# One transpose fewer a head, and the sums and states of the last hand-over taken up earlier, in the mLSTM layer of a two-layer decoder step

## The chip, the core and the metric

The kernel runs on one core of one Trainium2 chip. Its time is the device time in microseconds (us) of one execution. The time before is the median of 3 runs.

## The reference

One inference step of a two-layer decoder trunk, in float32, for a prompt of 256 tokens and 8 samples of 8 new tokens each (320 tokens in all, model width 1024). Layer 0 mixes tokens with a gated MLP in chunks of 128, layer 1 with an mLSTM matrix memory of 8 heads (key width 128, value width 256); each is followed by a gated MLP with a causal convolution. Only the mLSTM layer is touched. Per head `h` it computes, cut to what matters here:

```python
sc  = einsum('bhtd,bhsd->bhts', q, k) * w_intra
num = w_inter * einsum('bhtd,bhde->bhte', q, C) + einsum('bhts,bhse->bhte', sc, v)
den = w_inter * einsum('bhtd,bhd->bht', q, n) + sum(sc, axis=-1)
h   = num / maximum(abs(den), exp(-m_t))
C_new = decay * C + einsum('bhsd,bhse->bhde', k * g, v)
...
hn = (h - mean(h)) * rsqrt(var(h) + EPS) * gn_g
o  = sigmoid(o_pre)
y  = (o * hn) @ w_out
```

The prompt starts from an empty state, each sample from its own `C`, `n` and `m`; the new states are outputs as well.

## The kernel before

All activations lie transposed in SBUF: 128 partitions hold one block of 128 features, and the 320 tokens run along the free dimension (256 of the prompt, then 64 of the samples). A projection of one 128-wide block is 24 matmuls of 128x320: each weight block is split into a high and a low part (`wh` by ScalarE at L154, `wl` by VectorE at L155), and for each of 8 input blocks there are two products with `wh` and one with `wl`. In layer 1 the products with `wl` follow those with `wh` (`low_last`).

Layer 1 (`layer_b`) goes head by head, and the work of head `h-1` is laid between the projections of head `h`. An iteration of the loop holds in this order: the q block and its epilogue (`qk_epi`), the k block, the products of the samples' queries with their states (`inter`), the numerators of head `h-1` (`numer`), the first v block, the statistics of the numerators (`stats`, which end in `sl`, one over the standard deviation, made on GpSimd), the prompt's new state (`state_prompt`), two samples' new states (`state_sample(h-1, 0)`), the second v block, `state_sample(h-1, 1)`, `normed` (the normalised sums `hn`: (num - mean) * sl), `scores`, the two o blocks with `o_epi` (tanh of the output gate), `finish(h-1)` (transposes `hn`, makes `y_b` = (tanh + 1) * hn transposed, and splits it into `yhb` and `ylb`), the loads of the next states (`state_in`), their splits into `Ch` and `Cl` (`state_split`), and the transposes of k and v (`k_nat`, `v_nat`).

In `normed` and `finish`, `hn` is a tile of three groups of 128 token rows: two of the prompt and one whose lower 64 rows hold the samples and whose upper 64 rows are zeros. `finish` makes six transposes of 128x128, three for each half `e` of the head's 256 values, into two PSUM tiles named `phn`, and one `y_b` of 128x320 for each half.

The last iteration (`h = 7`, here "the last hand-over") has no o blocks in the loop: right behind `scores(7)` comes `finish(6)`, then products of the output projection (`begin(0)`, `begin(1)`), which use the finished heads, and `state_sample(6, 2)` and `(6, 3)`. Head 7's own o blocks, `stats`, `normed` and `finish(7)` stand behind the loop.

The order on TensorE is the order of the program: every matmul and transpose is pinned. The order on the other engines is laid out when the program is built, by a planner that knows the program order, the data and an estimate of each instruction's time. `tc.issue_after(ins)` makes every instruction traced in its block that runs on the engine of `ins` stand behind `ins` on that engine; it orders nothing else. Tiles come from pools with a fixed number of buffers; in PSUM `psm` has 3 (projections) and `psa` has 5 (`phn`, `num`, `pcs`, `psc`, `pCp`, `pv` and others), and a tile waits for a buffer until the last reader of the tile that held it is done.

Of the kernel before, what the change touches and what calls it, by code (L numbers as in the profile page):

```python
# [10 lines left out]
F32 = mybir.dt.float32  # L11
F32R = mybir.dt.float32r
AF = mybir.ActivationFunctionType
# [3 lines left out]
P = 128  # L17
EPS = 1e-6
TP = 256
# [6 lines left out]
NH = 8  # L26
# [11 lines left out]
class Net:  # L38
# [597 lines left out]
    def layer_b(self):  # L636
# [5 lines left out]
        with ExitStack() as ctx:  # L642
# [220 lines left out]
            def k_nat(h):  # L863
                s = S[h]
                ks = s["k"][0]
                pool, tag = (self.psm, "pm") if h < NH - 1 else (self.psa, "pa")
                pk = pool.tile([P, 512], F32, tag=tag, name="pk")
                for t in range(3):
                    self.tr(pk[:, t * P:(t + 1) * P], ks[:, t * P:(t + 1) * P], self.ident)
                kgh = hp.tile([P, 2, P], F32R, tag="kgh", name="kgh", bufs=1)  # L870
                kgl = hp.tile([P, 2, P], F32R, tag="kgl", name="kgl", bufs=1)
                kgs = hp.tile([P, 2, P], F32R, tag="kgs", name="kgs", bufs=1)
                kgz = hp.tile([P, NB, P], F32R, tag="kgz", name="kgz", bufs=1)
                g = colsT[:, 2, 32 + h:33 + h]
                src = pk[:, 2 * P:3 * P]

                for i, (r, o) in enumerate(((slice(0, 32), slice(32, 64)), (slice(32, 64), slice(0, 32)))):
                    nc.scalar.activation(kgs[:, i, :], src, AF.Copy, scale=g)
                    nc.vector.scalar_tensor_tensor(kgs[o, i, :], src[r], g[r], kgs[r, i, :].bitcast(F32), op0=MULT, op1=SUB)
                s["kg"] = (kgh, kgl, kgs, kgz)  # L880
                if h < NH - 1:
                    k_mask(h)
                for t in range(2):
                    g = colsT[:, t, 32 + h:33 + h]
                    src = pk[:, t * P:(t + 1) * P]
                    nc.scalar.activation(kgh[:, t, :], src, AF.Copy, scale=g)
                    nc.vector.scalar_tensor_tensor(kgl[:, t, :], src, g, kgh[:, t, :].bitcast(F32), op0=MULT, op1=SUB)
# [82 lines left out]
            def normed(h):  # L970
                src, mv, sl = S[h].pop("norm")
                nb = hp.tile([P, 3], F32, tag="nb", name="nb", bufs=1)
                made = nc.vector.scalar_tensor_tensor(nb, mv[:, :, 0], -1.0, sl, op0=MULT, op1=MULT)
                if h == NH - 1:
                    self.pin(made)
                for t in range(3):
                    n = P if t < 2 else 64
                    if h == NH - 1 and t:
                        nc.vector.tensor_scalar(hn[:n, t, :], src[t][:n, :DV], mv[:n, t, 0:1], sl[:n, t:t + 1], op0=SUB, op1=MULT)
                    else:  # L980
                        nc.scalar.activation(hn[:n, t, :], src[t][:n, :DV], AF.Identity, scale=sl[:n, t:t + 1], bias=nb[:n, t:t + 1])

            def state_prompt(h):
                s = S[h]
# [9 lines left out]
            def state_sample(h, i):  # L994
                s = S[h]
                kgz, dec, C0 = s["kg"][3], s["P"][2], s["C"][i]

                wide = h < NH - 2
                pcs = [pool.tile([P, 512], F32, tag=tag, name="pcs") for pool, tag in
                       ((self.psa, "pa"), (self.psm, "pm") if wide else (self.psa, "pa"))]  # L1000
                for u in range(2):
                    b = 2 * i + u
                    mm(pcs[u][:, :CW], kgz[:, b, :], vh[:, 2, :] if b < 4 else vb, True, True)
                for u in range(2):
                    b = 2 * i + u
                    made = nc.vector.scalar_tensor_tensor(C0[:, u, :], C0[:, u, :], dec[:, b:b + 1], pcs[u][:, :CW], op0=MULT, op1=ADD)  # L1006
                nc.sync.dma_start(O["Cs"][h, :, 2 * i:2 * i + 2, :], C0)
                return made

            def o_epi(h, j, ps):  # L1010
                o = lp.tile([P, T], F32, tag="ob", name="o_b", bufs=1)
                nc.vector.tensor_tensor(o, ps[:, :T], self.rb, op=MULT)  # L1012
                th = lp.tile([P, T], F32, tag="tho", name="th_o", bufs=4)
                nc.scalar.activation(th, o, AF.Tanh, scale=0.5)
                S[h].setdefault("o", []).append(th)

            def finish(h):
                s = S[h]
                yh = hp.tile([P, 2, T], F32R, tag="yhb", name="yhb", bufs=6)
                yl = hp.tile([P, 2, T], F32R, tag="ylb", name="ylb", bufs=6)  # L1020
                for e in range(2):
                    pt = self.psa.tile([P, 512], F32, tag="pa", name="phn")
                    for t in range(3):
                        self.tr(pt[:, t * P:(t + 1) * P], hn[:, t, e * P:(e + 1) * P], self.ident)
                    y = self.tp.tile([P, T], F32, tag="yf", name="y_b", bufs=2)
                    nc.vector.scalar_tensor_tensor(y, s["o"][e], 1.0, pt[:, :T], op0=ADD, op1=MULT)
                    g = gnh[:, 2 * h + e:2 * h + e + 1]
                    nc.scalar.activation(yh[:, e, :], y, AF.Copy, scale=g)
                    nc.vector.scalar_tensor_tensor(yl[:, e, :], y, g, yh[:, e, :].bitcast(F32), op0=MULT, op1=SUB)
                    Y[2 * h + e] = (yh[:, e, :], yl[:, e, :])  # L1030
# [11 lines left out]
            vb = hp.tile([P, CW], F32R, name="vb")  # L1042
            Qz = hp.tile([P, 8 * 136], F32R, name="Qz")
            Ps = hp.tile([P, P], F32R, name="Ps")
            hn = hp.tile([P, 3, DV], F32, name="hn")
            nc.gpsimd.memset(hn[64:, 2, :], 0.0)
            nc.gpsimd.memset(vh[:, :, DV:DV + 1].bitcast(F32), 1.0)
            nc.gpsimd.memset(vh[:, :, DV + 1:].bitcast(F32), 0.0)
            nc.gpsimd.memset(vl[:, :, DV:].bitcast(F32), 0.0)
# [10 lines left out]
            def blk():  # L1060
                return self.block(KD, self.x_rhs)

            part, done = {}, {}

            def begin(m):

# [7 lines left out]
            for h in range(NH):  # L1074
                if h:
                    rows_in(h)
                    qk_epi(h, 0, blk())
                    early(h, 0)
                    if h == 1:
                        inter(0, 0)  # L1080
                        state_split(0, 3)
                    inter(h - 1, 1)
                    qk_epi(h, 1, blk())
                    for i in (2, 3):
                        inter(h - 1, i)
                    numer(h - 1)
                    early(h, 1)
                    ps = blk()
                    with self.behind_split():
                        stats(h - 1)  # L1090
                    v_epi(h, 0, ps)
                    state_prompt(h - 1)
                    state_sample(h - 1, 0)
                    early(h, 2)
                    v_epi(h, 1, blk())
                if h:
                    made = state_sample(h - 1, 1)
                    with tc.issue_after(made.ins):
                        normed(h - 1)
                scores(h)  # L1100
                early(h, 3)
                last = h == NH - 1
                if h and not last:
                    o_epi(h, 0, blk())
                if last:
                    finish(h - 1)
                    begin(0)
                if h:
                    for i in (2, 3) if last else (2,):
                        state_sample(h - 1, i)  # L1110
                if last:
                    begin(1)

                    self.prefetch(0, self.used + 2)
                early(h, 4)
                if h:
                    state_in(h)
                    with tc.issue_after(made.ins):
                        for i in (0, 1):
                            state_split(h, i)  # L1120
                if h and not last:
                    o_epi(h, 1, blk())
                if h and not last:
                    finish(h - 1)
                    state_sample(h - 1, 3)
                k_nat(h)
                v_nat(h)
                if h:
                    inter(h, 0)
                    for i in (2, 3):  # L1130
                        low = state_split(h, i)
                else:
                    with tc.issue_after(self.parts[0].ins), tc.issue_after(self.parts[1].ins):
                        state_split(0, 2)
                early(h, 5)
# [184 lines left out]
```

## Time and profile before

| | |
|---|---|
| median of 3 runs | 955.47 us (955.44 to 955.82) |
| the profiled execution | 956.29 us, of which its span is 954.3 us |
| mean granted TensorE clock | 0.999 |
| TensorE busy | 946.0 us, 99% of the span |
| VectorE, ScalarE, GpSimd busy | 697.1, 531.0, 118.6 us |
| HBM traffic over the span | 162 GB/s |

The span runs from the first instruction to the last. A row of a timeline gives start, duration, engine, line, operation, destination and sources, how many like it are merged (xN), and in brackets how long the engine sat idle just before and what ended that. PE is TensorE's matmul, PEld its weight load, DVE VectorE, ACT ScalarE, POOL GpSimd, SPq the queue that issues DMAs.

### The profile page before, as it was taken

The page shows a single profiled execution, that of the slowest core. Times are in us where ns is not written, and L with a number is a line of the kernel's source. Part 1 is how long each engine was busy: PE and PEld are TensorE (multiplying, and loading weights), DVE is VectorE, ACT ScalarE, POOL GpSimd, SP SyncE. Part 2 cuts the span into 40 slices and gives each one's busy share as a digit, 9 for nine tenths or more (in the row PEclk, how much of TensorE's full clock was granted, in tenths as well). Part 3 has the DMA queues.
Part 4 walks back from the last instruction along what each step waited for, and adds up shares of the span by engine and source line. Part 5 has one row for each costly group of instructions (what it writes and reads, how often), then busy time and mean ns, then how long its engine had stood idle before and what let it go on. Part 6 is the DMA issues. An engine that isn't in the chain of part 4 may idle for free.

```text
span 954.3 us, 17083 instructions
## 1 busy us (share of the span) xinstructions
PE 946.0 (99%) x6420; PEld 932.1 (98%) x6420; DVE 697.1 (73%) x1324; ACT 531.0 (56%) x978; POOL 118.6 (12%) x291
## 2 busy tenths in 40 slices
PE   9999999999999999999999999999999999999997
PEld 8889999999999999999999999999999999999997
DVE  5866976577777764559999998887897777775443
ACT  6657443454554443348877767666766445544342
POOL 3200000010000000014432312202001000000000
PEclk9999999999999999999999999999999999999999
DMA  8643346444444454465465756654474444445441
GB/s 262 208 162 134 129 135 202 162 141 149 153 156 151 138 160 155 146 216 175 155 198 191 222 167 205 198 188 129 123 241 155 150 145 152 155 146 154 143 141 55
DMA packets 55237, 156.13 MB, mean 164 GB/s; under 512 B 7492, under 2 KB 13132, under 8 KB 55156
## 3 DMA queue, kind: packets, MB, share of 16 engines
q1 hardware_dynamic: 55156, 155.06, 50.2%
q8 instruction: 50, 0.82, 0.3%
q14 instruction: 31, 0.25, 0.1%
HBM read 143.05 MB, written 11.99 MB: 162 GB/s over the span
## 4 chain that ended last, share of the span: by engine, by line
PE 92%; DVE 4%; ACT 2%; issue 1%; DMA 1%; SPq 0%; POOL 0%; ACTq 0%
PE pm L54 80%; PE pv_a L54 5%; PE num L54 2%; PE pmix L54 1%; DVE wl L155 1%; PE pcs L54 1%; DMA raw<-in_a_wv 1%; PE pCp L54 1%; PE phn L57 0%; ACT wh L154 0%; PE pv L57 0%; PE psc L54 0%; PE pc L54 0%; DVE C L1006 0%; DVE dg L291 0%
## 5 line engine op out<-in xcount | busy, mean ns | idle before, releaser
L154 ACT CAST wh<-raw 128x1024 fp32r<-128x1024 f32 (+3 forms) x256 | 256.7, 1004 | 276.6 <-PE pm L54 147.8
L155 DVE TENSOR_TENSOR wl<-raw,wh 128x1024 fp32r<-128x1024 f32 (+3 forms) x256 | 299.0, 1169 | 125.7 <-ACT wh L154 121.5
L54 PE MATMUL pm<-xh,wh 128*128 128x320 f32 x1216 | 372.2, 311 | 0.2 <-DVE o_b L1012 0.2
L54 PE MATMUL pm<-xl,wh 128*128 128x320 f32 x1216 | 370.2, 309 | 0.0
L54 PE MATMUL pm<-xh,wl 128*128 128x320 f32 x1216 | 321.2, 309 | 0.0
L54 PEld LDWEIGHTS pm<-xh,wh 128*128 128x128 f32 x1216 | 228.4, 188 | 0.6 <-DVE o_b L1012 0.4
L54 PEld LDWEIGHTS pm<-xl,wh 128*128 128x128 f32 x1216 | 228.4, 188 | 0.2
L54 PEld LDWEIGHTS pm<-xh,wl 128*128 128x128 f32 x1216 | 214.5, 188 | 0.0
L54 PE MATMUL pm<-yh_f,wh 128*128 128x320 f32 x352 | 108.8, 309 | 0.0
L54 PE MATMUL pm<-yl_f,wh 128*128 128x320 f32 x352 | 108.8, 309 | 0.0
L54 PE MATMUL pm<-yh_f,wl 128*128 128x320 f32 x352 | 108.8, 309 | 0.0
L54 PEld LDWEIGHTS pm<-yh_f,wh 128*128 128x128 f32 x352 | 66.1, 188 | 0.0
L54 PEld LDWEIGHTS pm<-yl_f,wh 128*128 128x128 f32 x352 | 66.1, 188 | 0.0
L54 PEld LDWEIGHTS pm<-yh_f,wl 128*128 128x128 f32 x352 | 66.1, 188 | 0.0
L532 DVE SCALAR_TENSOR_TENSOR fcv<-fpad,vecs,fcv 128x336 f32<-128x336 f32 x88 | 49.6, 566 | 2.1 <-ACT fcv L530 0.7
L54 PE MATMUL pm<-yh_a,wh 128*128 128x320 f32 x128 | 39.6, 310 | 0.0
L54 PE MATMUL pm<-yh_a,wl 128*128 128x320 f32 x128 | 39.5, 309 | 0.0
L54 PE MATMUL pm<-yl_a,wh 128*128 128x320 f32 x128 | 39.5, 309 | 0.0
L534 ACT ACTIVATE fgl<-fcv 128x256 f32<-128x256 f32 x44 | 18.3, 415 | 37.8 <-DVE fcv L532 37.8
L54 PE MATMUL pm<-yhb,wh 128*128 128x320 f32 x128 | 38.1, 311 | 0.0
L54 PE MATMUL pm<-ylb,wh 128*128 128x320 f32 x128 | 37.9, 309 | 0.0
L304 DVE TENSOR_TENSOR xT<-pm,xT 128x320 f32<-128x320 f32 x39 | 19.0, 488 | 25.0 <-PE pm L54 24.9
(289 smaller groups left out, 1368.3 us busy)
## 6 DMA issues: line engine op xcount, KB each, us to landing
raw<-in_f_up SPq DMA_DIRECT2D x88, 512.0 KB, 3.2
raw<-in_b_win SPq DMA_DIRECT2D x48, 512.0 KB, 3.9
raw<-in_f_dn SPq DMA_DIRECT2D x32, 448.0 KB, 3.3
C<-in_C SPq DMA_DIRECT2D x32, 258.0 KB, 3.8
out_Cs<-C SPq DMA_DIRECT2D x32, 258.0 KB, 3.8
raw<-in_a_win SPq DMA_DIRECT2D x16, 512.0 KB, 3.2
raw<-in_a_wo SPq DMA_DIRECT2D x16, 512.0 KB, 4.0
raw<-in_f_dn SPq DMA_DIRECT2D x16, 512.0 KB, 3.5
```

The costliest lines, as they stand in the source:

```text
L54: self.pin(self.nc.tensor.matmul(out, lhsT, rhs, start=start, stop=stop, skip_group_check=skip))
L154: self.last_split = self.hold(nc.scalar.copy(wh[:, :kn, :], raw[:, :kn, :]))
L155: self.last_low = nc.vector.tensor_tensor(wl[:, :kn, :], raw[:, :kn, :], wh[:, :kn, :].bitcast(F32), op=SUB)
L304: self.nc.vector.tensor_tensor(x, ps[:, :T], x, op=ADD)
L532: nc.vector.scalar_tensor_tensor(cv, pd[:, i:i + NC], self.vec(w + i * KF), cv, op0=MULT, op1=ADD)
L534: nc.scalar.activation(gl[:, :TP], cv[:, :TP], AF.Gelu_apprx_tanh)
```

## The change

- The samples' normalised sums go to a tile of their own, `hs`, in which the two halves `e` lie one under the other (64 rows each), so that one transpose turns both; `hn` keeps the two prompt groups. The write of the samples' sums becomes two instructions of 64x128 instead of one of 64x256. `finish` makes four transposes into one PSUM tile and one into another. The zeroing of `hn`'s upper rows goes.
- `y_b` becomes one tile for both halves, made by one instruction over 128x(2x256) for the prompt and one over 128x(2x64) for the samples. The two tanh tiles of a head become one.
- In the last iteration `normed(6)` moves up behind `state_sample(6, 0)`, ordered behind its last VectorE instruction; `state_in(7)` and the first two `state_split(7, ...)` follow there, the latter's VectorE part behind `nb` (L973). Both stand ahead of `state_sample(6, 1)` and `scores(7)`.
- In iterations from the third on, the VectorE instructions traced in the k block (the low part `wl` of a later weight block) stand behind the last `y_b`.
- Head 0's transposed k goes to a `psa` tile instead of a `psm` tile.

```diff
-                pool, tag = (self.psm, "pm") if h < NH - 1 else (self.psa, "pa")
+                pool, tag = (self.psm, "pm") if 0 < h < NH - 1 else (self.psa, "pa")
...
-                for t in range(3):
-                    n = P if t < 2 else 64
-                    if h == NH - 1 and t:
-                        nc.vector.tensor_scalar(hn[:n, t, :], src[t][:n, :DV], mv[:n, t, 0:1], sl[:n, t:t + 1], op0=SUB, op1=MULT)
+                last = h == NH - 1
+                for t in range(2):
+                    if last and t:
+                        nc.vector.tensor_scalar(hn[:, t, :], src[t][:, :DV], mv[:, t, 0:1], sl[:, t:t + 1], op0=SUB, op1=MULT)
                     else:
-                        nc.scalar.activation(hn[:n, t, :], src[t][:n, :DV], AF.Identity, scale=sl[:n, t:t + 1], bias=nb[:n, t:t + 1])
+                        nc.scalar.activation(hn[:, t, :], src[t][:, :DV], AF.Identity, scale=sl[:, t:t + 1], bias=nb[:, t:t + 1])
+
+                for e in range(2):
+                    a, z = hs[64 * e:64 * e + 64, :], src[2][:, e * P:(e + 1) * P]
+                    if last:
+                        nc.vector.tensor_scalar(a, z, mv[:64, 2, 0:1], sl[:64, 2:3], op0=SUB, op1=MULT)
+                    else:
+                        nc.scalar.activation(a, z, AF.Identity, scale=sl[:64, 2:3], bias=nb[:64, 2:3])
+                return made
...
             def finish(h):
...
+                pt, ps = [self.psa.tile([P, 512], F32, tag="pa", name="phn") for _ in range(2)]
                 for e in range(2):
-                    pt = self.psa.tile([P, 512], F32, tag="pa", name="phn")
-                    for t in range(3):
-                        self.tr(pt[:, t * P:(t + 1) * P], hn[:, t, e * P:(e + 1) * P], self.ident)
-                    y = self.tp.tile([P, T], F32, tag="yf", name="y_b", bufs=2)
-                    nc.vector.scalar_tensor_tensor(y, s["o"][e], 1.0, pt[:, :T], op0=ADD, op1=MULT)
+                    for t in range(2):
+                        self.tr(pt[:, (2 * e + t) * P:(2 * e + t + 1) * P], hn[:, t, e * P:(e + 1) * P], self.ident)
+                self.tr(ps[:, :P], hs, self.ident)
+                yb = lp.tile([P, 2, T], F32, name="y_b", bufs=1)
+                o = s["o"]
+                for c, n, x in ((slice(0, TP), TP, pt), (slice(TP, T), 64, ps)):
+                    self.y_made = nc.vector.scalar_tensor_tensor(yb[:, :, c], o[:, :, c], 1.0, x[:, :2 * n].rearrange("p (e t) -> p e t", e=2), op0=ADD, op1=MULT)
+                for e in range(2):
+                    y = yb[:, e, :]
...
-            nc.gpsimd.memset(hn[64:, 2, :], 0.0)
...
+            def states(h, made):
+
+                state_in(h)
+                with tc.issue_after(made.ins):
+                    for i in (0, 1):
+                        state_split(h, i)
...
                     inter(h - 1, 1)
-                    qk_epi(h, 1, blk())
+                    if h > 1:
+                        with tc.issue_after(self.y_made.ins):
+                            ps = blk()
+                    else:
+                        ps = blk()
+                    qk_epi(h, 1, ps)
...
-                    state_sample(h - 1, 0)
+                    made = state_sample(h - 1, 0)
                     early(h, 2)
                     v_epi(h, 1, blk())
+                last = h == NH - 1
+                if last:
+                    with tc.issue_after(made.ins):
+                        made = normed(h - 1)
+                    states(h, made)
                 if h:
                     made = state_sample(h - 1, 1)
-                    with tc.issue_after(made.ins):
-                        normed(h - 1)
+                    if not last:
+                        with tc.issue_after(made.ins):
+                            normed(h - 1)
                 scores(h)
...
-                if h:
-                    state_in(h)
-                    with tc.issue_after(made.ins):
-                        for i in (0, 1):
-                            state_split(h, i)
+                if h and not last:
+                    states(h, made)
```

More of the change, by code (lines that the diff above doesn't have):

```diff
@@ L1012, in o_epi @@
                 nc.vector.tensor_tensor(o, ps[:, :T], self.rb, op=MULT)
-                th = lp.tile([P, T], F32, tag="tho", name="th_o", bufs=4)
-                nc.scalar.activation(th, o, AF.Tanh, scale=0.5)
-                S[h].setdefault("o", []).append(th)
+                if not j:
+                    S[h]["o"] = lp.tile([P, 2, T], F32, tag="tho", name="th_o", bufs=2)
+                nc.scalar.activation(S[h]["o"][:, j, :], o, AF.Tanh, scale=0.5)
             def finish(h):
@@ L1044, in layer_b @@
             Ps = hp.tile([P, P], F32R, name="Ps")
-            hn = hp.tile([P, 3, DV], F32, name="hn")
-            nc.gpsimd.memset(hn[64:, 2, :], 0.0)
+            hn = hp.tile([P, 2, DV], F32, name="hn")
+            hs = hp.tile([P, P], F32, name="hs")
             nc.gpsimd.memset(vh[:, :, DV:DV + 1].bitcast(F32), 1.0)
@@ L1092, in layer_b @@
                     state_prompt(h - 1)
-                    state_sample(h - 1, 0)
+                    made = state_sample(h - 1, 0)
                     early(h, 2)
                     v_epi(h, 1, blk())
+                last = h == NH - 1
[3 more added lines that the diff above has]
+                    states(h, made)
                 if h:
                     made = state_sample(h - 1, 1)
-                    with tc.issue_after(made.ins):
-                        normed(h - 1)
+                    if not last:
+                        with tc.issue_after(made.ins):
+                            normed(h - 1)
                 scores(h)
                 early(h, 3)
-                last = h == NH - 1
                 if h and not last:
```

## The prediction, made before the change was run

> **What bounds the kernel now.** I read the page first, then the waits of TensorE's weight loads, the chain that ended last, and the timeline around each wait that the change can touch.
>
> ```profile
> PE 946.0 (99%) x6420; PEld 932.1 (98%) x6420; DVE 697.1 (73%) x1324; ACT 531.0 (56%) x978; POOL 118.6 (12%) x291
> PE 92%; DVE 4%; ACT 2%; issue 1%; DMA 1%; SPq 0%; POOL 0%; ACTq 0%
> PEld phn L57 <- ACT hn L981: 1.8, 3, 1.2
> PEld num L54 <- DVE y_b L1026: 0.5, 1, 0.5
> PEld pm L54 <- DVE o_b L1012: 0.4, 1, 0.4
> ```
>
> TensorE is the bound over nearly the whole span, and its order is fixed. So an edit pays only where it takes work off TensorE or one of these three waits (total us, times, longest). The first is the last hand-over; here is its timeline:
>
> ```profile
> 663.16 0.88 DVE L1006 SCALAR_TENSOR_TENSOR C<-C,Mb,pcs 128x258 f32<-128x258 f32 x2
> 663.32 0.85 POOL L964 TENSOR_TENSOR sl<-t,mhalf 128x3 f32<-128x3 f32 x1 [4.70 <-DVE t L962]
> 665.96 0.41 ACT L154 CAST wh<-raw 128x256 fp32r<-128x256 f32 x1 [2.54 <-PE pm L54]
> 666.85 0.42 DVE L155 TENSOR_TENSOR wl<-raw,wh 128x256 fp32r<-128x256 f32 x1 [2.67 <-ACT wh L154]
> 667.09 0.53 PEld L54 LDWEIGHTS psc<-qs 128*128 128x128 f32 x4
> 667.20 0.87 DVE L1006 SCALAR_TENSOR_TENSOR C<-C,Mb,pcs 128x258 f32<-128x258 f32 x2
> 668.17 1.02 ACT L981 ACTIVATE hn<-num,nb,sl 128x256 f32<-128x256 f32 x2 [0.84 <-DVE nb L973]
> 668.65 1.28 DVE L911 TENSOR_TENSOR Cl<-C,Ch 128x516 fp32r<-128x516 f32 x2
> 668.79 0.14 PEld L57 LDWEIGHTS phn<-ident,hn 128*128 128x128 f32 x1 [1.17 <-ACT hn L981]
> 669.24 0.14 PEld L57 LDWEIGHTS phn<-ident,hn 128*128 128x128 f32 x1 [0.32 <-ACT hn L981]
> 669.73 0.42 PEld L57 LDWEIGHTS phn<-ident,hn 128*128 128x128 f32 x4 [0.35 <-ACT hn L981]
> ```
>
> TensorE has loaded its last scores weight at 667.62 and stands for 1.17 + 0.32 + 0.35 = 1.84 us until `hn` arrives piece by piece. `hn` needs `sl`, there at 664.17, and `nb`, which is queued behind the second pair of C; yet VectorE had sat idle for 2.67 us and ScalarE for 2.54 us before that.
>
> **Part by part.** *Last hand-over.* Behind the first C pair (done 664.04), `nb` can run at 664.2 and ScalarE can make `hn` and `hs` from 664.4. Two operations of 0.5 us (1.02 for the pair above) and two of about 0.36 (the 128x128 row below) end near 666.1. That lies in ScalarE's idle time but for 0.15 us, by which the `wh` at 665.96 may slip. The transposes can then start at 667.62 without a wait: **-1.84 us**. Of the states that move, the loads are long issued, the `Ch` casts are ordered behind nothing new, and the two `Cl` (1.28 us of VectorE) fall into its 2.67 us of idle time; if they didn't, they would stand where they stand now. The output DMA that is passed stays behind its own C.
>
> ```profile
> 645.19 0.33 SPq L903 DMA_DIRECT2D C<-in_C  x1
> L878 ACT ACTIVATE kgs<-pk,cols 128x128 fp32r<-128x128 f32 x12 | 4.3, 360 | 0.7 <-DVE kgs L879 0.2
> L981 ACT ACTIVATE hn<-ns,nb,sl 64x256 f32<-64x256 f32 x6 | 3.6, 595 | 0.0
> 473.23 0.59 ACT L981 ACTIVATE hn<-ns,nb,sl 64x256 f32<-64x256 f32 x1
> 505.18 0.66 PE phn L57 x6
> L57 PE MATMUL phn<-ident,hn x48: 271/272/328, 476.2 to 688.4; 128*128 128x128 f32 x48
> ```
>
> *Transposes.* In the chain, six take 0.66 us of TensorE's time: 0.11 each. Eight go, one a head; head 0's stands ahead of the wait at 478.46 (below) and vanishes in it, so 7 x 0.11 = **-0.77 us**. The duration of one is 272 ns because they overlap, and is not its price. The Trainium skill (TensorE: Matmul & The Clock Gate, Part 4: PE-mode transpose) gives about 275 ns for a transpose in a kernel's context; the duration here agrees, but charged for each it would make this term 1.93 us and the sum -3.5 us. The chain's spacing decides for 0.11.
>
> *`hs` in two pieces.* 2 x 0.36 in place of 0.595 is 0.13 us more ScalarE a head, hidden because `hn` is ready ahead of its transposes: in iteration 1 at 473.82, when the first of them runs at 476.2. Uncovered it would cost just that. In `finish(7)` the two pieces run on VectorE ahead of the `hn` of ScalarE, and no wait of `phn` but that of the hand-over is in the list above.
>
> *`y_b` by parts.* The first instruction now spans 512 elements:
>
> ```profile
> L1026 DVE SCALAR_TENSOR_TENSOR y_b<-th_o,phn 128x320 f32<-128x320 f32 x14 | 6.3, 479 | 0.2 <-PE phn L57 0.2
> L832 DVE SCALAR_TENSOR_TENSOR Pf<-psc,w 128x384 f32<-128x384 f32 x5 | 2.8, 551 | 0.0
> L911 DVE TENSOR_TENSOR Cl<-C,Ch 128x516 fp32r<-128x516 f32 x24 | 15.5, 682 | 0.0
> 477.94 0.87 DVE L1026 SCALAR_TENSOR_TENSOR y_b<-th_o,phn 128x320 f32<-128x320 f32 x2
> 478.46 0.19 PEld L54 LDWEIGHTS num<-Ch,Qz 128*128 128x128 f32 x1 [0.50 <-DVE y_b L1026]
> 505.70 0.88 DVE L1026 SCALAR_TENSOR_TENSOR y_b<-th_o,phn 128x320 f32<-128x320 f32 x2
> 507.06 0.48 PE num L54 x4
> ```
>
> Between 551 (384 elements) and 682 ns (516) it takes 0.68, not 0.48 us. The first `num` of the next head waits for the buffer that this instruction reads. In iteration 1 that wait already decides, so `num` comes **+0.20 us** later. In the heads after it `y_b` would end at 505.70 + 0.68 = 506.38, and `num` starts at 507.06: covered, by over 0.4 us after the 0.11 of TensorE's lead and 0.11 for loading weights.
>
> *Head 0.* With k's transposes in `psa`, the 0.40 us wait on `o_b` goes. VectorE is 28.96 us busy in the 30 us from 449 to 479, so what is late next is the same `num` at 478.46. Credit between -0.40 and 0; I take 0, as VectorE's backlog doesn't start at that wait. The dropped zeroing is on that backlog:
>
> ```profile
> 449.00:479.00 30.00, 29.57 (x214) 29.08 (x213) 28.96 (x73) 25.01 (x62) 14.14 (x28) 1.00 0.44 152
> 448.09 0.31 POOL L1046 MEMSET hn<- 64x256 f32 x1 [3.21 <-PE psc L54]
> 451.54 0.56 DVE L832 SCALAR_TENSOR_TENSOR Pf<-psc,w 128x384 f32<-128x384 f32 x1 [0.21 <-POOL w L813]
> ```
>
> GpSimd heads its queue with it, and VectorE waits 0.21 us for that queue: between -0.21 and 0, I take **-0.10**.
>
> *Behind the hand-over* TensorE is 1.95 us earlier (1.84 + 0.11). Can VectorE follow?
>
> ```profile
> 673.03 1.65 DVE L1006 SCALAR_TENSOR_TENSOR C<-C,Mb,pcs 128x258 f32<-128x258 f32 x4
> 675.11 0.19 PEld L54 LDWEIGHTS num<-Ch,Qz 128*128 128x128 f32 x1
> 671.00:684.00 13.00, 13.00 (x99) 12.99 (x99) 12.39 (x32) 11.35 (x31) 0.79 (x1) 1.00 0.24 73
> 688.65 0.47 ACT L1014 ACTIVATE th_o<-o_b 128x320 f32<-128x320 f32 x1 [1.36 <-DVE o_b L1012]
> 690.58 0.55 DVE L1029 SCALAR_TENSOR_TENSOR ylb<-y_b,gnh,yhb 128x320 fp32r<-128x320 f32 x1
> 692.07 0.31 PE L54 MATMUL pm<-ylb,wh 128*128 128x320 f32 x1
> ```
>
> From 668.05, where its second C pair ends now as before, VectorE loses 1.28 of `Cl`, 0.15 of `nb` (half of it overlapped: 0.07) and the wait for the late `phn`, some 0.16 us: 1.51. Head 7's first `num` needs the third of these four C (two buffers go to `pv`), which ends at 674.27, 0.84 ahead. That leaves 0.84 - 1.95 + 1.51 = 0.40 us: nothing is taken, 0 to +0.7 is kept (rival 1).
>
> *finish(7).* Both halves of `y_b` now wait for head 7's second tanh (there at 689.12), where the first half went ahead. The second `y_b`, 128 elements, is about 0.25 us by the slope of the rows above (1.0 to 1.1 ns an element below 479 at 320). 689.12 + 0.68 + 0.25 gives `y_b` at 690.05; two casts and two low parts in turn (0.55 each, pairwise overlapped) the last `ylb` at about 691.7, against 691.13 now. Its use moves up to 691.96. A C fits before `y_b`, but the low weights queued behind `ylb` come late by up to half a us: 0 to +0.5, I take **+0.15**. The Trainium skill (Perfetto Trace Analysis, Optimizing Scalar/DVE Operations) says that breaking up instructions may complete work sooner where they cause bubbles; the merge does the reverse, and by that rule the upper end would hold and the sum be -2.0.
>
> The ordering of `wl` behind `y_b` has no price in itself: what is ordered has its use two blocks later.
>
> **Sum:** -1.84 - 0.77 + 0.20 - 0.10 + 0.15 = -2.36 us. The profiled execution (956.29: span 954.3 and 1.99 around it) would become 953.93, the median, which lies 0.82 lower, 955.47 - 2.36 = **953.1**.
>
> **Rivals.** *1. The gain is partly given back* (0.20). VectorE and ScalarE are refilled by the planner. If the low part of 0.42 us and one more `Cl` (0.68) come before the four C, the 0.40 us of slack turns into a 0.70 us wait; with finish(7) at its +0.5 the sum is -2.36 + 0.70 + 0.35 = -1.31: 954.2. For it: VectorE is 12.39 us busy in the 13 us from 671 to 684. Against: C stands earlier in the program than the splits.
>
> *2. It doesn't do what it says* (0.12). The new order is only a lower bound for `nb`; if it is laid no earlier than now, the 1.84 us stay and -0.77 + 0.20 - 0.10 + 0.15 = -0.52 is left: 954.9. Against: VectorE and ScalarE have nothing else to do from 664.2 to 665.9.
>
> *3. Slower* (0.12). The change holds back only the low part traced in the k block. If one traced in the q block, 1.22 us long, were laid between `o_b` and `y_b` in the five heads after the first, it would outlast the 0.46 us of cover by 0.76 each time: -2.36 + 5 x 0.76 = +1.4: 956.9. It decides from 0.46 us of delay on. Against it: this instruction now ends 0.6 us before `o_b`:
>
> ```profile
> 503.47 1.22 DVE L155 TENSOR_TENSOR wl<-raw,wh 128x1024 fp32r<-128x1024 f32 x1
> 505.29 0.49 DVE L1012 TENSOR_TENSOR o_b<-pm,rb 128x320 f32<-128x320 f32 x1 [0.60 <-PE phn L57]
> ```
>
> **How the numbers follow.** My forecast has 0.56. Its own bounds, with the terms at their ends, are -1.84 - 0.77 - 0.40 - 0.21 = -3.2 and about -1.9: 952.2 to 953.6. The range takes in rivals 1 and 2: 952.2 to 955.0, leaving out rival 3 and the tails. Within 0.2% (1.9 us, about what a measurement of this kernel can tell from no change) means 953.56 to 957.38. Faster beyond it: most of the forecast and a little of rival 1, 0.58. Within: the rest of rival 1, rival 2 and half of rival 3, 0.34. Slower: the rest of rival 3, if it hits more heads, 0.08.
>
> **What would show it.** The wait of `phn` on `hn` gone, `hn` on ScalarE before its `wh` near 666; five transposes in 0.55 us; a `num` wait of 1.0 to 1.2 us on `y_b` in iteration 1 (it swallows the 0.51 us lead); no wait of `num` on C in iteration 7. I am wrong if `hn` still ends after 668, if `num` waits in every head, or if the output projection waits for `ylb` or its low weights by more than half a us.

## The result, and the profile after

The changed kernel takes 959.60 us in the median of 6 runs (958.25 to 961.40), the kernel before beside it 955.46 (955.25 to 955.91). The ratio is 1.004, with a 95% interval of 1.003 to 1.005: slower, where 953.1 was forecast. The profiled execution of the changed kernel took 961.40 us with a span of 958.8, 4.5 us more than the span before.

First the busy row and the chain that ended last, from the page after:

```profile
PE 947.2 (99%) x6412; PEld 933.1 (97%) x6412; DVE 696.7 (73%) x1325; ACT 533.6 (56%) x985; POOL 115.9 (12%) x290
PE 87%; DVE 7%; ACT 3%; issue 1%; DMA 1%; POOL 0%; SPq 0%; ACTq 0%; DVEq 0%
```

TensorE has its eight instructions fewer (6412 for 6420), yet its share of the chain fell from 92 to 87%, and VectorE's rose from 4 to 7%. Where that is, the waits of TensorE's weight loads between 430 and 720 us say (total us, times, longest):

```profile
PEld num L54 <- DVE y_b L1037: 4.8, 4, 2.1
PEld pcs L54 <- POOL bpad L761: 1.4, 1, 1.4
PEld pm L54 <- DVE wl L155: 0.6, 1, 0.6
PEld num L54 <- DVE Cl L911: 0.2, 1, 0.2
PEld psc L54 <- DVE khl L312: 0.2, 1, 0.2
```

The wait of `phn` on `hn` is gone, as forecast, and so is that of `pm` on `o_b`. In their place `num` waits for `y_b` in four iterations instead of one, and `pcs` (the products for the samples' new states) waits once. Four readings follow.

**The hand-over did what it was meant to do.** The first three rows are of the timeline after, the last of the chain after:

```profile
670.24 0.16 DVE L973 SCALAR_TENSOR_TENSOR nb<-mv,sl 128x3 f32<-128x3 f32 x1 [0.17 <-POOL sl L964]
670.44 1.02 ACT L981 ACTIVATE hn<-num,nb,sl 128x256 f32<-128x256 f32 x2 [0.98 <-DVE nb L973]
671.35 0.99 ACT L988 ACTIVATE hs<-ns,nb,sl 64x128 f32<-64x128 f32 x2
673.79 0.55 PE phn L57 x5
```

`nb` follows `sl` at once, all sums are there at 672.34, and the five transposes run at 673.79 without a wait, in 0.55 us. (Rows of this part of the profile after lie some 6 us later than before, by the waits and the low clock told of below.)

**A low part between `o_b` and `y_b`.** In iterations 4, 5 and 6 the planner now lays one there. The chain after, in iteration 4, and below it the same place in the timelines of iterations 5 and 6:

```profile
564.22 0.47 DVE o_b L1020
564.70 1.13 DVE wl L155
565.83 0.61 DVE y_b L1037
566.49 0.75 PE num L54 x4
567.23 12.09 PE pm L54 x72
```

```profile
605.81 1.21 DVE L155 TENSOR_TENSOR wl<-raw,wh 128x1024 fp32r<-128x1024 f32 x1
606.94 0.88 DVE L1037 SCALAR_TENSOR_TENSOR y_b<-th_o,phn 128x512 f32<-128x512 f32 x2
607.67 0.19 PEld L54 LDWEIGHTS num<-Ch,Qz 128*128 128x128 f32 x1 [0.85 <-DVE y_b L1037]
645.46 1.21 DVE L155 TENSOR_TENSOR wl<-raw,wh 128x1024 fp32r<-128x1024 f32 x1
647.32 0.19 PEld L54 LDWEIGHTS num<-Ch,Qz 128*128 128x128 f32 x1 [0.85 <-DVE y_b L1037]
```

The first `num` of the next head waits behind it 2.1, 0.85 and 0.85 us. Before, `y_b` followed `o_b` directly in every head. In iterations 4 to 6 `early(h, 5)` lays two blocks of the output projection, over finished heads, behind the last o block; the three low parts are traced in the second of them (a block makes the low part of the block after it). The change's ordering covers the k block alone, whose low part it keeps away in iterations 1 to 3.

**The exps ahead of their data.** In iteration 4 ScalarE stands for the row `Mb` from HBM; first the rows before, then those after:

```profile
541.04 0.67 ACT L768 ACTIVATE bcv<-bpad,vecs 128x344 f32<-128x344 f32 x1
543.24 1.04 ACT L811 ACTIVATE w<-Mb,cols 128x256 f32<-128x256 f32 x3 [1.52 <-DMA Mb<-rows]
```

```profile
543.97 1.04 ACT L811 ACTIVATE w<-Mb,cols 128x256 f32<-128x256 f32 x3 [4.53 <-DMA Mb<-rows]
545.69 0.66 ACT L768 ACTIVATE bcv<-bpad,vecs 128x344 f32<-128x344 f32 x1
549.72 0.40 ACT L861 CAST vh<-vh 32x256 fp32r<-32x256 f32 x1
550.24 0.30 PEld L54 LDWEIGHTS pcs<-vh,kgz 128*128 128x128 f32 x2 [1.42 <-POOL bpad L761]
```

The planner has put these exps ahead of a `Ch`, a `kgh` and a `bcv`, which the kernel before takes up while the row is still on its way. What is queued behind the stand comes late. `pcs` waits 1.4 us; the list names GpSimd's `bpad`, but `pcs` doesn't read that. It reads `vh`, whose last piece ScalarE ends at 550.12, 0.12 us before the weight load (and 0.12 us before it in the profiles of e1, e7 and e12 too). `o_b` of this iteration comes late as well, which is part of the 2.1 above (0.5 to 1 us of it, by e1 and e2 below). A stand need not cost anything: before the change ScalarE stood 4.64 us for the row of iteration 5, and no wait of TensorE followed.

**Low weights at the end.** The output projection behind `finish(7)` waits 0.59 us for a low part that VectorE takes up behind a residual:

```profile
697.85 0.55 DVE L233 SCALAR_TENSOR_TENSOR xl<-xT,vecs,xh 128x320 fp32r<-128x320 f32 x1
698.32 0.41 DVE L155 TENSOR_TENSOR wl<-raw,wh 128x256 fp32r<-128x256 f32 x1
698.79 0.30 PEld L54 LDWEIGHTS pm<-yhb,wl 128*128 128x128 f32 x2 [0.59 <-DVE wl L155]
```

In all, the waits on `y_b` grew by 4.3 us, and 1.4 + 0.6 + 0.2 + 0.2 came new: 6.7. Against them stand 1.84 and 0.40 for waits that went and 0.88 for eight transposes, which leaves 3.6 us. The clock cost 1.5 us more in this execution (last section), and its first scores, with all that stands ahead of them in layer 0, which the change does not touch, ran 0.8 us sooner than those before:

```profile
446.96 0.36 PE L54 MATMUL psc<-qh,kh 128*128 128x256 f32 x1
```

```profile
446.14 0.36 PE L54 MATMUL psc<-qh,kh 128*128 128x256 f32 x1
```

That makes 4.3 of the 4.5 us by which the span grew.

### The profile page after: what moved, and what is told of

Same layout as the page of the kernel before. It is cut to its first block, busy times and chain, and to the rows that moved or that the text cites. A ratio compares the mean times of both kernels' runs of the same rounds, so it can differ in the third digit from the quotient of the medians.

```text
span 958.8 us, 17086 instructions
## 1 busy us (share of the span) xinstructions
PE 947.2 (99%) x6412; PEld 933.1 (97%) x6412; DVE 696.7 (73%) x1325; ACT 533.6 (56%) x985; POOL 115.9 (12%) x290
## 4 chain that ended last, share of the span: by engine, by line
PE 87%; DVE 7%; ACT 3%; issue 1%; DMA 1%; POOL 0%; SPq 0%; ACTq 0%; DVEq 0%
PE pm L54 75%; PE pv_a L54 6%; PE num L54 2%; DVE wl L155 2%; PE pmix L54 1%; DVE C L1014 1%; DMA Mb<-rows 1%; ACT wh L154 1%; ACT Ch L910 0%; DVE y_b L1037 0%; DVE o_b L1020 0%; DVE bcv L770 0%; PE pcs L54 0%; PE pCp L54 0%; PE pc L54 0%
```

## The experiments

Each ratio is to the kernel before on the same chip, whose median was 956.39 us beside the first four kernels, 956.23 beside the next four, 956.15 beside the three after them and 955.91 beside the last. The lists of waits are of 430 to 720 us throughout; the rows that matter are shown, and each list is of one execution. In the code, `...` stands for what is left out.

**e1, the second output block ordered too.** The kernel after, with:

```diff
 def early(h, r):
-    for m in self.EARLY_OUT.get((h, r), ()):
-        self.residual(m, self.block(8, lambda k: Y[k]))
+    for i, m in enumerate(self.EARLY_OUT.get((h, r), ())):
+        with ExitStack() as es:
+            if r == 5 and i:
+                es.enter_context(tc.issue_after(self.y_made.ins))
+            ps = self.block(8, lambda k: Y[k])
+        self.residual(m, ps)
```

> The changed kernel, with the VectorE work traced in the second of the two output-projection blocks at the end of iterations 4, 5 and 6 ordered behind y_b as well; it brings the 1.21 us low part back behind y_b there, and lays the exps of heads 5 to 7 (which read a row loaded by DMA) ahead of k's second cast. Theory A (the loss is this low part between o_b and y_b): the waits of num on y_b in iterations 4 to 6 (2.1 + 0.85 + 0.85 us in the changed kernel) lose 1.2 + 0.85 + 0.85 = 2.9 us, and the lower TensorE clock behind the 2.1 us wait goes: 959.6 becomes 956 to 957. Theory B (the loss is ScalarE standing 4.5 us before the exps of heads 3 and 4 for the row's DMA, with all that is queued behind them): the wait of pcs of 1.4 us in iteration 4 stays, the like of it may come up in iterations 5 to 7, and the time stays above 958.

956.43 us, ratio 0.9997 (0.9988 to 1.0005):

```profile
PEld num L54 <- DVE y_b L1037: 2.9, 3, 1.0
PEld pcs L54 <- issue: 0.5, 1, 0.5
```

The waits of 0.85 us in iterations 5 and 6 are gone, and that of iteration 4 is down from 2.1 to 0.97: the rest of it comes from ScalarE, which stands 3.32 us there. The third wait, 0.98 us, is in iteration 3, where the change's profile had none: ScalarE stands 3.11 us for the row there in this execution, 1.48 in that one. 0.4% of the time is won back by this one ordering, as theory A expected.

**e2, the exps behind the convolution.** The kernel after, with the exps of heads 3 and 4 behind the first convolution operation of the q block on ScalarE:

```diff
-nc.scalar.activation(cv, ...)
+s["cv" + str(j)] = nc.scalar.activation(cv, ...)
...
+with ExitStack() as es:
+    if h in WAFTER:   # (3, 4)
+        es.enter_context(tc.issue_after(s["cv0"].ins))
     nc.scalar.activation(w[...], pb[...], AF.Exp, ...)
```

> The changed kernel, with the exps of heads 3 and 4 ordered behind the first convolution step of q on ScalarE, where they stood before; the low part stays ahead of y_b in iterations 4 to 6. Theory A: 1.21 us of low part still stands before y_b in three iterations, so waits of num of about 0.85 us each stay (2.5 us): not below 957.5. Theory B: the waits of pcs (1.4) and psc (0.2) in iteration 4 go and num's wait there falls from 2.1 to about 0.9, 2.8 us in all, and no wait is long enough for the lower clock: 955.5 to 957.

957.20 us, ratio 1.0008 (0.9999 to 1.0017):

```profile
PEld num L57 <- DVE y_b L1043: 4.4, 4, 1.6
PEld pm L57 <- DVE wl L158: 0.6, 1, 0.6
```

The waits of `pcs` and `psc` are gone, as theory B has it, the two of 0.85 us stay, as A has it, and iteration 4's wait is 1.65 us: the stand and the low part each make a part of it. The time lies between the two forecasts.

**e3, both.** As e1 and e2, with the exps of heads 3 to 7.

> Both orders: the low part behind y_b as in the first of these, and the exps of heads 3 to 7 behind q's first convolution step. If A and B together are the loss, no wait of num on y_b is left but iteration 1's (1.0 us), none of pcs, and the clock stays up: 953.1 to 954.0, as was predicted for the change itself. If the merged y_b or the five transposes cost something by themselves, it stays above 955.

954.35 us, ratio 0.9975 (0.9965 to 0.9986):

```profile
PEld num L57 <- DVE y_b L1043: 1.0, 1, 1.0
PEld pm L57 <- DVE wl L158: 0.6, 1, 0.6
```

With the two orders alone the change is faster than the kernel before. The time is 0.35 us above the range that was expected; the 0.6 us on low weights, which stayed, were not in it. No `num` waits for `y_b` behind iteration 1.

**e4, the hand-over alone.** The kernel before with the moved `normed(6)`, `state_in(7)` and splits, and nothing else of the change.

> The kernel before, with the last hand-over's part alone (normed(6) and the states of head 7 moved up); six transposes, y_b by halves. By the prediction's step the wait of phn on hn (1.84 us) goes and nothing else moves: 955.46 - 1.84 = 953.6. If the gain is given back behind the hand-over (num waiting for C, or the output projection for ylb), 954.2 to 955.

954.30 us, ratio 0.9976 (0.9967 to 0.9985):

```profile
PEld num L54 <- DVE y_b L1027: 0.5, 1, 0.5
PEld pm L54 <- DVE o_b L1013: 0.4, 1, 0.4
```

The 1.84 us are worth 2.3 here, with neither a low part nor the exps out of place. So both come from the other parts of the change; and e3, which has the five transposes besides, is no faster: by the lists of waits their 0.88 us were lost to 0.6 us of low weights, 0.5 us more in iteration 1 and 0.2 on `Cl`, less the 0.4 on `o_b` that went.

**e5, `y_b` by halves.** The kernel after, with the instruction over both halves undone, the five transposes kept:

```diff
-for c, n, x in ((slice(0, TP), TP, pt), (slice(TP, T), 64, ps)):
-    self.y_made = nc.vector.scalar_tensor_tensor(yb[:, :, c], o[:, :, c], 1.0, x[:, :2 * n].rearrange("p (e t) -> p e t", e=2), op0=ADD, op1=MULT)
+for e in range(2):
+    nc.vector.scalar_tensor_tensor(yb[:, e, :TP], o[:, e, :TP], 1.0, pt[e][:, :TP], op0=ADD, op1=MULT)
+self.y_made = nc.vector.scalar_tensor_tensor(yb[:, :, TP:], o[:, :, TP:], 1.0, pt[1][:, TP:TP + P].rearrange("p (e t) -> p e t", e=2), op0=ADD, op1=MULT)
```

Each half's two transposes go to a tile of their own, the samples' one behind those of the second half.

> The kernel after, with only the making of y_b changed back to halves: each half of the prompt has a PSUM tile and an instruction of 128x256 of its own, the samples of both halves one of 128x(2x64); still five transposes, and the hand-over as in the change. Theory (it is the merge of y_b over both halves that let the planner lay a low part of 1.21 us between the gate's o_b and y_b: the merged one needs four transposes, and the estimates leave a hole there): with halves the low part stays ahead of o_b in every head, so the three waits of num on y_b of 2.1, 0.85 and 0.85 us go, but for the part of the 2.1 that comes from ScalarE's stand (up to 1 us); the wait in iteration 1 falls from 1.0 to about 0.5 us, and the 0.6 us wait on the low weights behind the last ylb goes too; the 1.4 us wait of pcs stays. From 959.6: -2.8 -0.5 -0.6 = about 955.7, and less where the clock no longer drops. Rival (the order on VectorE has shifted because of the hand-over or the ordering in the k block, whatever y_b looks like): the three waits stay, and about 958.5 results.

954.52 us, ratio 0.9985 (0.9976 to 0.9994):

```profile
PEld pm L54 <- DVE wl L155: 1.1, 1, 1.1
PEld num L54 <- DVE y_b L1037: 1.0, 2, 0.7
```

No new ordering is in this kernel, and the low part is out of the gap in all heads. So it is the merge that opened the gap, not the hand-over, the five transposes or the ordering, which this kernel has too. The `pcs` wait, which was expected to stay, is gone as well: the exps fell into another order, and ScalarE's stand in iteration 4 shrank to 2.30 us:

```profile
541.88 0.51 ACT L811 ACTIVATE w<-Mb,cols 128x256 f32<-128x256 f32 x1 [2.30 <-DMA Mb<-rows]
```

The wait on low weights, expected to go, grew to 1.1 us and moved to a later block. The time is 1.2 us below what was expected, about as much as `pcs` no longer waits; that the one makes the other is only argued.

**e6, halves and exps ordered.**

> y_b by halves as in the run before, with the exps of heads 3 to 7 behind the convolution's first operation of the q block on ScalarE and the second output-projection block ordered behind y_b, as in the run e3. Theory (the change's savings are real, 1.84 us for the hand-over and 0.88 us for the transposes, and what ate the latter in e3 was the wider y_b: 0.5 us more in iteration 1 and 0.6 us on the low weights at the end): both waits go, so the time is that of e3 less about 1.1 us, 953.3, the best of all. Rival (transposes hide behind VectorE in these stages, which is as late as before): the same as e3 or as the hand-over alone, 954.3.

954.08 us, ratio 0.9978 (0.9968 to 0.9987):

```profile
PEld pm L57 <- DVE wl L158: 1.1, 1, 1.1
PEld num L57 <- DVE y_b L1043: 0.7, 1, 0.7
```

The time is the rival's: the wait in iteration 1 and that on the low weights remained.

**e7, without the change's own ordering.** The kernel after, with the k block traced plainly.

> The kernel after without the ordering of the k block's VectorE work behind y_b. Theory (the merge opens the hole in every head, and that ordering closes it in the heads 1 to 3, where the low part comes from the k block): a low part stands between o_b and y_b in six heads, num waits about 0.85 us in each, and the time is that of the change plus about 3 x 0.85 = 2.5 us, 962. Rival (the ordering itself pushes the low parts into the hole, later by half a block): without it the waits in iterations 4 to 6 go, and the time falls to about 956.

963.92 us, ratio 1.0081 (1.0067 to 1.0094):

```profile
PEld num L54 <- DVE y_b L1037: 8.2, 6, 2.6
PEld pcs L54 <- issue: 1.7, 1, 1.7
```

The low part stands in the gap in six heads. The ordering in the change is a remedy for its own merge that reaches half of the places; without it some 4 us more are lost. 2.5 were expected, from three more waits of 0.85 us; in iterations 1 and 3 they were longer.

**e8, one wait left alone.** As e1, but iteration 4's second output block is not ordered.

> The kernel after, with the second output-projection block of iterations 5 and 6 ordered behind y_b, but not that of iteration 4, so that the wait of about 2.1 us stands alone. Theory (the clock of TensorE drops for some us behind a wait of this length): the time is that of the change less 2 x 0.85 = 957.9; the granted clock of TensorE over the 10 us behind the wait is again near 0.6 in the first 3.6 us, and against the run e1, which has a wait of about 1 us at that place, the kernel is slower by 1.1 us for the wait and up to 1.5 us for the clock, in the executions in which the clock drops. Rival (the low clock in the profile of the change was chance): the clock stays at 1.00 behind the wait, and the difference to e1 is 1.1 us, 957.5.

957.25 us (955.74 to 959.37), ratio 1.0012 (1.0003 to 1.0021). The wait is there, and the granted clock behind it is full (the column before the last two of the second row):

```profile
565.62 0.19 PEld L54 LDWEIGHTS num<-Ch,Qz 128*128 128x128 f32 x1 [2.09 <-DVE y_b L1037]
```

```profile
568.00:572.00 4.00, 4.00 (x29) 4.00 (x29) 3.90 (x9) 2.59 (x6) 2.04 (x2) 1.00 0.79 262
```

So a wait of this length need not drop the clock. The time can't tell the theory (957.9) from its rival (957.5): the interval takes in both. It lies 0.8 us above e1 by the medians, 0.15% by the ratios.

**e9, low weights first.** e6 with one order more:

```diff
-self.residual_norm(m, ps, V_FFN + 8)
+with ExitStack() as es:
+    if m in (1,):
+        self.prefetch(0, self.used + 2)
+        es.enter_context(tc.issue_after(self.last_low.ins))
+    self.residual_norm(m, ps, V_FFN + 8)
```

`prefetch` makes the high and low parts of the next blocks ahead of their use, and the VectorE work of the second block's residual stands behind the last low part.

> The run e6 (y_b by halves, exps behind the convolution) with one order more: behind finish(7), the low part of the output projection's fourth block is made ahead of the second block's residual on VectorE. Theory (e6 keeps one wait that is not there before the change, 1.1 us of the output projection on that low part, since VectorE takes up residuals and new states first): the wait goes, and with it 1.1 us of e6's time, 954.1 to 953.0, against 956.2 before. Rival (what stands behind the wait is the DMA of the next weights, or the residuals, which wait next): 0.5 us or less is gained, 953.6 to 954.1.

953.27 us, ratio 0.9972 (0.9962 to 0.9982), and beside this only the 0.2 us on `Cl` are left in the list of waits:

```profile
PEld num L57 <- DVE y_b L1043: 0.7, 1, 0.7
```

So the wait of 1.1 us is gone. The gain on e6 is 0.6 us by the ratios and 0.7 by the medians, each against its kernel before, less than the 1.1 of the theory.

**e10, the same with the merged `y_b`.** e3, with that order at `m` = 0 and 1.

> The run e3 (y_b over both halves as in the change, with the second output-projection block ordered behind y_b and the exps behind the convolution) with the low parts made ahead of the residuals of the first two blocks of the output projection. Theory: the 0.6 us wait of pm on wl goes, 954.35 to 953.75; the 1.0 us wait in iteration 1 stays, so it ends up to half a us behind the version by halves. Rival (merge and halves are then the same, since VectorE, and not the form of y_b, sets when num starts in iteration 1): the two kernels agree within 0.2 us.

953.36 us, ratio 0.9970 (0.9958 to 0.9981), the rival's outcome: both forms are equally fast. In iteration 1 the merged form waits 1.0 us, the halves 0.7, and the times can't tell them apart:

```profile
PEld num L57 <- DVE y_b L1043: 1.0, 1, 1.0
```

The wait on low weights is gone here too. These two are the best of all, about 0.3% under the kernel before.

**e11, transposes without hand-over.** e9 with the old hand-over.

> The run e9 with the last hand-over as it is before the change: hn and the states of head 7 where they stood. Theory (hand-over and transposes add up): TensorE waits for hn again, in pieces, 1.84 us in all, and the time is that of e9 plus 1.84, some 955.0 to 955.2, about 1.0 us below the kernel before. Rival (the transposes' 0.77 us are always lost to VectorE, which is the bound of these stages): the time is that of the kernel before, 956.2, and the gain of e9 against the hand-over alone is nothing.

955.41 us, ratio 0.9993 (0.9984 to 1.0002):

```profile
PEld phn L60 <- ACT hn L987: 1.5, 2, 1.2
PEld phn L60 <- ACT hs L994: 0.6, 1, 0.6
```

With the hand-over as before, TensorE waits 2.1 us for `hn` and `hs`, and the time is 2.14 us above e9. The transposes bring 0.7 us by the medians, with the repairs of e9 beside them; the interval just includes no change.

**e12, the change once more.**

> The kernel after, unaltered, once more and on another chip, for the clock behind its 2.1 us wait in iteration 4. Theory (a wait of this length drops the clock in some executions and not in others, since in the run e8 the same wait left it at 1.00): the executions spread over some 3 us, as they did (958.3 to 961.4), the profiled one has either 3.6 us at about 0.6 behind that wait or a full clock throughout, and in the latter case its span is about 957 and not 958.8. Rival (the drop belongs to this kernel's order, the spread to something else): the drop is there again at the same place, whatever the span.

959.40 us (958.12 to 960.44), ratio 1.0033 (1.0022 to 1.0045). The clock was 1.00 throughout in this profile; its span was nevertheless 958.2. `num` waited in five iterations here, all waits of the list come to 7.5 us (7.2 in the first profile), and the first scores ran 0.4 us later than in that profile:

```profile
PEld num L54 <- DVE y_b L1037: 5.8, 5, 2.1
```

The theory's 957 was missed. The fifth wait, 0.97 us, is in iteration 3, as in e1, and the row landed 6.0 us after its issue there, where it took 4.45 in the change's first profile, so that ScalarE stood for it 3.20 us instead of 1.48. In iteration 4 it stood 3.39 instead of 4.53, and `pcs` waited 0.5 us instead of 1.4. So what a stand costs differs from one execution of a program to the next. Beside e1, whose stand in iteration 4 is as long (3.32 us) and whose wait is 0.97, the 2.1 us here give the price of the low part alone there: 1.1 us.

## Why the prediction was wrong

**Hand-over, -1.84:** right, and shown by itself at -2.1 (e9 against e11) to -2.3 (e4). The piece of `hs` was mis-sized: it takes 0.49 us, not 0.36, which the new hand-over covers; with the old one TensorE waits 2.1 us (e11).

**Transposes, 0.11 each:** right in the trace (five in 0.55 us). Of the -0.77 forecast the times show 0.7, at the edge of what they can tell (e11).

**Head 0, 0, and iteration 1, +0.20:** right. The wait on `o_b` (0.4) went, one of 0.2 on `Cl` came, and that of `num` grew from 0.5 to 1.0, at the edge of the 1.0 to 1.2 announced. GpSimd's 0.10 can't be told apart. `y_b` itself was sized right: 0.675 us for 512 elements (0.68 forecast). The samples' 128 elements took 0.276, where 0.25 was written; the slope of the rows it named gives 0.27 to 0.29.

**`finish(7)`, +0.15:** mis-sized. The mechanism was named, low weights queued behind `ylb`, with an end of 0.5; the wait measured 0.6 us, and e10 removed it.

**The step that failed** is "In the heads after it `y_b` would end at 505.70 + 0.68 = 506.38, and `num` starts at 507.06: covered". It gave the longer `y_b` its old place in VectorE's order. But the planner lays that order anew from when an instruction's inputs are there by its estimates. The old first half needed three transposes, the merged one four. With it a 1.21 us low part got in ahead of `y_b`; in e5, without the merge, it did not, and e1 and e7 show its price. Where the order is kept, the step holds: in e3 and e10 no `num` waits behind iteration 1. That the planner saw a gap as long as the fourth transpose is only argued; that the merge causes it is shown. Rival 3, with 0.12, had this mechanism and its price in a head (0.76, measured 0.85 where VectorE has time to spare ahead of `o_b`, 1.1 in iteration 4). Its time, 956.9, is 2.7 us short of the measured one: it had five heads where three were hit, and neither ScalarE nor the clock. It looked for the low part in the q block only. "The ordering of `wl` behind `y_b` has no price in itself" is borne out by e7, which is slower without it, and beside the point: the ordering was in the diff, and the question it should have raised is which other blocks' low parts can come to the same place.

**Not foreseen at all** was ScalarE: with the change the planner lays the exps of a head ahead of work that could run while their row is on its way. Which part of the change moves them is not shown; in e5, without the merge, they lie in a third order. By the ratios against 1.004, putting the exps back is worth 0.3% of the time (e2), keeping the low part away 0.4% (e1), and both together 0.65% (e3).

**The other rivals** did not come: `nb` follows `sl` at once (rival 2), and `num` waits for no C in iteration 7 (rival 1).

Taken with both repaired and the low weights first, the change gives -0.28 to -0.30% (e9 and e10), 2.7 to 2.8 us against the -2.36 forecast. In the lists of waits, 2.7 us before become 1.2 in e10, and eight transposes make 0.88: 2.4 in all. So the terms were nearly right for TensorE, though the small ones are below what the times can tell, and the loss came from two queues that the sum held fixed.

## What to carry to other kernels

Where a planner lays the order of the engines, an edit that makes an instruction depend on more has a price that no term for its duration holds: look for the longest instruction that is free to run at that time and reckon it into the gap, once for every block that can supply one. If a change carries an ordering that holds something back, ask what it is a remedy for, and whether it reaches every place.

## What the runs showed of the hardware

TensorE's clock fell behind a wait of 2.1 us in one execution and not in another of the same program, nor in e8. The windows behind that wait, of the change's first profile and, below, of its second (length, busy time and count for TensorE, its weight loads, VectorE, ScalarE, GpSimd, then the granted clock, the DMA share and GB/s):

```profile
566.40:570.00 3.60, 3.52 (x16) 3.52 (x17) 3.47 (x10) 2.63 (x6) 1.15 (x2) 0.62 0.87 300
570.00:580.00 10.00, 10.00 (x69) 10.00 (x68) 5.70 (x12) 5.44 (x11) 2.14 (x6) 0.97 0.56 175
```

```profile
570.00:580.00 10.00, 10.00 (x71) 10.00 (x70) 5.73 (x11) 6.02 (x13) 2.97 (x6) 1.00 0.57 198
568.19 10.56 PE pm L54 x72
```

In the first, the 72 matmuls behind the wait took 12.09 us (the last row of the chain shown above), in the second 10.56: the low clock cost 1.5 us. The Trainium skill (TensorE: Matmul & The Clock Gate, Part 1) has the clock fall after an idle window of some 3.4 us and calls the window free-running: it doesn't restart with the kernel. That the same wait drops the clock in one execution only agrees with a free-running window; that a whole window must be idle is not what this trace shows, as TensorE stood for 2.1 us here. Whether this also makes the spread of the change's runs (958.25 to 961.40) is not shown: in e7, whose longest wait is 2.6 us, the clock was again low behind it, at 0.66 over 4 us, while e8 spreads as widely with a full clock in its profile:

```profile
480.00:484.00 4.00, 3.76 (x18) 3.76 (x19) 3.84 (x11) 2.64 (x6) 1.38 (x2) 0.66 0.74 266
```

A ScalarE operation of 64x128 with a scale and a bias read from memory takes 0.49 us, against 0.595 for 64x256 before: halving the row saves a sixth.
